# A seven-product output projection: its operand sums and the last gating bound to the order of the text, and one quad's modulation products a step sooner

## The chip, the cores and the metric

The kernel runs on one core of a Trainium2 chip. Its time is device microseconds (us) of one execution; 876.02 us is the median of three (876.01 to 876.03). The engines are PE (matrix products), DVE and ACT (element-wise work), POOL (here only DMA with accumulation) and SP (here only loads).

## The reference, cut to what matters

The input is 512 latent tokens and 256 context tokens of width 1024. Layer 0 is bidirectional retention with 4 heads, layer 1 a chunked gMLP; each is modulated by products of a conditioning vector with `ada_w`. Everything is float32. The change touches layer 0:

```python
def retention_output(o, z, w_out):                    # o: a head's scores times v, z: its gate
    o = o * lax.rsqrt(jnp.mean(o * o, axis=-1, keepdims=True) + NORM_EPS)
    o = o.transpose(0, 2, 1, 3).reshape(b, l, h * dv).astype(z.dtype)
    return (o * jax.nn.silu(z)) @ w_out
...
shift_x, scale_x, gate_x = jnp.split(silu_c @ ada_w[i] + ada_b[i], 3, axis=-1)
...
x = x + gate_x[:, None] * out_x
```

A head has 256 columns of q and k and 512 of v and z. The score of each pair of tokens is multiplied by a power of the head's decay before it meets v.

## The kernel before, in words

**Products in float32.** PE multiplies in a reduced form, so every operand is split: ACT casts it to its high half, DVE subtracts that from it to get the low half (`split`), and `mm3` adds three products (low x high, high x low, high x high). A weight tile of 1024 columns costs one ACT CAST and one DVE subtraction (hl<-raw); halves lie in four `hl` tiles, so that the preparation of weights runs two products ahead of their use (`Q.get`).

**Seven products in place of eight.** Large weights are multiplied in quads: a matrix is cut in 2 x 2, and seven products of sums replace eight of parts (`PAIRED` and `SINGLE` give their order). Weight sums T1 and T2 are made by DVE (raw<-raw), T3 and T4 by an accumulating DMA on POOL's queue. The other operand of each product is A11, A12, A22 or one of the sums S1 to S4; in the output projection of heads 0 and 1, tags stand for them: A11 in oS3, A12 in oA12, A22 in oA22, S1 in oA11, S2 in oS1, S4 in oS2, S3 in oS4. `PAIRED` there is B11 (with A11), B21 (A12), T1 (S1), T2 (S2), B22 (S4), T3 (S3), T4 (A22), each for two column pairs in turn: fourteen works, numbered n = 0 to 13. Each is a block of 24 records of 256 columns on PE. A block's result is read by `Product`: snapshots (snap) by ACT, additions to them by DVE.

**Order.** `Queue` wraps an engine: PE runs in the order of the text throughout. ACT and DVE are ordered freely by the scheduler, but inside a `pinned` stretch each instruction comes after the one before it in the text, and after a `fence` nothing later passes it. `aside(work)` runs one step of a generator pinned: such steps are loads with their halves (`load_qk`, `load_v`, `load_wo`), the decay tables (`decay`), and `step`, the next step of `background`. That one makes four vectors of modulation in turn (`ada_piece`: eight rows ada<-adag are loaded into `bg` tiles, and DVE adds each, times a number, to `ada_a`); `columns` then multiplies ada_a with ones on PE, ACT copies the result out (cole), PE transposes it. A PSUM bank has the tag "ps" (six banks) or "tm" (two).

**Attention** (`attend`): for each head, half of the tokens and pair of key blocks, a score (12 products in a tm bank), its decay (pf on DVE), its halves (ph, pl), and two steps later the products with v. `finish` squares and takes the root on ACT, `gated` multiplies with the gate on DVE (gt), `flip` transposes the gated block on PE, and `turn` makes the operands from it. Heads 0 and 1 go together (`attend_two`): a quarter of the 2 x 2 cut comes from each half. The last gated block is flipped inside the second block of the projection (`out_two`, after half of its products), and quarter_22 makes S1, S2, S4 and A22 from it at once. Heads 2 and 3 are done one by one (`attend_one`, `project_out`).

`between_modes` is one product of ones with ones between transpositions and the next products; PE shows it as two records.

The z quad of head 2 is the sixth quad (n = 5) of the loop over `QUADS[3:]`; at its products i in the step table (L1198) `step` runs.

## Time and profile before

| what | before |
|---|---|
| median of three runs | 876.02 us |
| the profiled execution | 875.56 us |
| its span in the profile | 873.8 us |
| clock of PE granted, mean | 0.995 |
| PE busy 350 to 400, 400 to 450, 450 to 500 us | 49.46, 47.33, 47.43 of 50 us |
| granted clock in the same | 1.00, 0.97, 1.00 |
| DVE busy in the same | 45.91, 34.03, 41.10 us |

The span lies inside the time of the execution; 1.76 us of the execution lie outside it. A timeline row gives start, duration, engine, what is written and read, the shape and the number of instructions; in brackets stand the idle time before it and the instruction that ended it. The projection of heads 0 and 1 takes 380.7 to 425.8 us, head 2 and its projection 426 to 476, head 3 what comes then.

### The profile page before, as it was taken

How to read it: one execution, taken by the hardware profiler on the slowest of the kernel's cores; microseconds unless marked ns; L12 is line 12 of the kernel's file. 1: busy time of each engine (PE TensorE's matmuls, PEld its weight loads, DVE VectorE, ACT ScalarE, POOL GpSimd, SP SyncE). 2: the span in 40 equal slices, each digit the busy share in tenths (PEclk: the TensorE clock that was granted, in tenths of full speed). 3: DMA queues.
4: the chain of work that ended last, by engine and by line, in shares of the span. 5: the costliest groups of instructions: out<-in, count | busy, mean ns of one | idle time of the engine just before them, and what ended most of it. 6: DMA issues, size and time to landing. Idle time of an engine off the chain costs nothing.

```text
span 873.8 us, 17037 instructions
## 1 busy us (share of the span) xinstructions
PE 856.6 (98%) x6820; PEld 818.0 (94%) x6820; DVE 709.4 (81%) x1003; ACT 479.9 (55%) x757; POOL 84.8 (10%) x127
## 2 busy tenths in 40 slices
PE   8999999999999999999999999999999999999996
PEld 7899999999999999889989899999999899899985
DVE  4799899969968875897677879998888478678895
ACT  5466544464355346657672549744666456255434
POOL 0001211211211010010100002021000000000110
PEclk9999999999999999999999999999999999999998
DMA  9945867868967796258984642657555246146532
GB/s 360 403 122 151 248 193 270 254 201 242 303 188 223 232 337 199 87 151 272 239 288 150 217 105 109 203 148 236 175 146 191 51 146 203 39 145 194 121 48 97
DMA packets 78126, 167.96 MB, mean 192 GB/s; under 512 B 8160, under 2 KB 33248, under 8 KB 78048
## 3 DMA queue, kind: packets, MB, share of 16 engines
q1 hardware_dynamic: 65280, 126.30, 43.4%
q0 software_dynamic: 12336, 40.38, 18.3%
q8 instruction: 53, 0.87, 0.4%
q10 hardware_dynamic: 432, 0.20, 0.1%
q14 instruction: 25, 0.20, 0.1%
HBM read 128.58 MB, written 24.12 MB: 175 GB/s over the span
## 4 chain that ended last, share of the span: by engine, by line
PE 81%; DVE 8%; DMA 7%; ACT 2%; issue 1%; DVEq 0%; SPq 0%; ACTq 0%
PE pst L54 81%; DMA ada_w<-in_ada_dram 2%; DVE hl L54 2%; DMA cq<-in_cT_dram 1%; DVE v L54 1%; DMA bg<-in_adag_dram 1%; DVE gt L54 1%; DMA qk<-q 1%; DMA bg<-in_dec_dram 1%; DVE ada_a L54 1%; DMA vt<-vt 1%; DVE quarter L54 1%; DMA raw<-in_w_dram 1%; DVE pf L54 0%; DMA cv<-in_cv_dram 0%
## 5 line engine op out<-in xcount | busy, mean ns | idle before, releaser
L54 DVE TENSOR_TENSOR hl<-raw,hl 128x1024 fp32r<-128x1024 f32 (+2 forms) x203 | 242.5, 1199 | 71.8 <-ACT hl L54 71.3
L54 ACT CAST hl<-raw 128x1024 fp32r<-128x1024 f32 (+2 forms) x203 | 208.3, 1031 | 155.7 <-PE pst L54 70.6
L54 PE MATMUL pst<-oS,hl 128*128 128x256 f32 x1296 | 157.4, 280 | 2.3 <-DVE hl L54 1.8
L54 PEld LDWEIGHTS pst<-oS,hl 128*128 128x128 f32 x1296 | 152.5, 190 | 3.6 <-DVE hl L54 2.1
L54 PE MATMUL pst<-hl,oS 128*128 128x256 f32 x1152 | 134.4, 276 | 0.0
L54 PE MATMUL pst<-oA,hl 128*128 128x256 f32 x1080 | 134.3, 280 | 0.1
L54 PEld LDWEIGHTS pst<-hl,oS 128*128 128x128 f32 x1152 | 132.3, 188 | 0.8 <-ACT hl L54 0.4
L54 PEld LDWEIGHTS pst<-oA,hl 128*128 128x128 f32 x1080 | 127.8, 188 | 2.0 <-ACT oS L54 0.4
L54 PE MATMUL pst<-hl,oA 128*128 128x256 f32 x768 | 92.4, 277 | 0.0
L54 DVE TENSOR_TENSOR raw<-raw 128x1024 f32<-128x1024 f32 x73 | 88.8, 1219 | 0.8
L54 PEld LDWEIGHTS pst<-hl,oA 128*128 128x128 f32 x768 | 89.4, 188 | 0.0
L54 ACT ACTIVATE snap<-pst 128x512 f32<-128x512 f32 x81 | 48.2, 595 | 63.3 <-PE pst L54 63.2
L54 PE MATMUL pst<-v,ph 128*128 128x512 f32 x192 | 59.8, 393 | 0.0
L54 PE MATMUL pst<-hl,ya 128*128 128x512 f32 (+1 forms) x246 | 59.1, 386 | 0.0
L187 POOL DMA_DIRECT2D raw<-raw x27 | 23.5, 869 | 365.1 <-DVE raw L54 145.5
L54 DVE TENSOR_TENSOR snap<-snap,pst 128x512 f32<-128x512 f32 x75 | 51.0, 680 | 6.2 <-PE pst L54 5.9
L54 PEld LDWEIGHTS pst<-hl,ya 128*128 128x128 f32 x246 | 45.3, 188 | 9.5
L54 PE MATMUL pst<-og,hl 128*128 128x256 f32 x384 | 46.6, 280 | 0.0
L54 PEld LDWEIGHTS pst<-og,hl 128*128 128x128 f32 x384 | 45.0, 188 | 0.4 <-DVE og L54 0.3
L54 PEld LDWEIGHTS pst<-v,ph 128*128 128x128 f32 x192 | 36.1, 188 | 7.1
L54 PEld LDWEIGHTS pst<-qk 128*128 128x128 f32 x288 | 35.8, 188 | 3.9 <-DVE pf L54 2.8
L54 PE MATMUL pst<-qk 128*128 128x256 f32 x288 | 36.8, 280 | 2.6 <-DVE pf L54 2.6
(222 smaller groups left out, 1085.6 us busy)
## 6 DMA issues: line engine op xcount, KB each, us to landing
raw<-in_w_dram SPq DMA_DIRECT2D x224, 256.0 KB, 3.8
bg<-in_adag_dram SPq DMA_DIRECT2D x32, 512.0 KB, 4.9
raw<-raw POOLq DMA_DIRECT2D x27, 512.0 KB, 5.1
ada_w<-in_ada_dram SPq DMA_DIRECT2D x16, 512.0 KB, 9.1
raw<-in_w_dram SPq DMA_DIRECT2D x16, 512.0 KB, 4.4
bg<-in_dec_dram SPq DMA_DIRECT2D x12, 512.0 KB, 5.1
v<-snap POOLq DMA_DIRECT2D x16, 256.0 KB, 4.4
z<-snap POOLq DMA_DIRECT2D x16, 256.0 KB, 4.6
```

What stands on the lines that cost most here:

```text
L54: made = op(*args, **kw)
L187: nc.gpsimd.dma_start(self.raws[q, to], self.raws[q, src], accum_op=ALU.add)
```

## The change

The last quarter of the seven-part projection is no longer made at once when its block is flipped: quarter_22 becomes a generator `sums`, whose four steps run pinned behind the works n = 1 (S1), 3 (S2), 5 (S4) and 6 (A22). The last gating is pinned and fenced (`bound`), and the weights that are made `ahead` of the projection are pinned too. `between_modes` moves into every flip. Head 2's decay goes to other tags and starts at n = 7; the last two halves of its v run in its own attention (`own`). The rows of the last modulation vector (i = 3) come into three tiles, loaded two ahead, and one step of `background` more is taken in the first half of head 2's projection, one less in head 3's attention. In the z quad of head 2 the second of three steps runs behind the third product instead of the fourth.

```diff
@@ -976,13 +976,13 @@
 
     row_tags = ["g0", "s3"]
 
-    def ada_piece(i, tag, tags):
+    def ada_piece(i, tag, tags, ahead=1):
         a = st([P, D], tag, name="ada_a")
         rows = []
         for k in range(KT + 1):
-            if k < KT:
+            for j in range(len(rows), min(k + ahead, KT)):
                 rows.append(bg_raw(tags))
-                load(rows[k], adag_d[8 * i + k])
+                load(rows[j], adag_d[8 * i + j])
             if k == 0:
                 yield None
                 continue
@@ -1016,7 +1016,7 @@
     def background():
         for i in range(4):
             a = None
-            for a in ada_piece(i, *(("g1", row_tags) if i < 3 else ("oA22", ("w2", "w3")))):
+            for a in ada_piece(i, *(("g1", row_tags) if i < 3 else ("oA22", ("w2", "w3", "g1"), 2))):
                 if a is None:
                     yield
             yield
@@ -1051,12 +1051,16 @@
 
     bg = background()
 
+    def bound(work):
+
+        before = act.pinned
+        act.pinned = dve.pinned = True
+        r = work()
+        act.pinned = dve.pinned = before
+        return r
+
     def aside(work):
-
-        act.pinned = dve.pinned = True
-        r = next(work, None)
-        act.pinned = dve.pinned = False
-        return r
+        return bound(lambda: next(work, None))
 
     def step():
         return aside(bg)
@@ -1195,7 +1199,7 @@
                 popped()
             if (n, i) in ((0, 3), (0, 5), (1, 0), (1, 2)):
                 aside(ctx_sum)
-            if 2 not in pieces and i in {0: (2, 4, 6), 1: (1, 3, 5, 6), 2: (1, 3, 5), 3: (0, 2, 4, 6), 5: (1, 3, 5), 6: (1, 3, 5)}.get(n, range(7)):
+            if 2 not in pieces and i in {0: (2, 4, 6), 1: (1, 3, 5, 6), 2: (1, 3, 5), 3: (0, 2, 4, 6), 5: (1, 2, 5), 6: (1, 3, 5)}.get(n, range(7)):
                 pieces.append(step())
             if n == 3 and i % 2:
                 aside(dec0)
@@ -1270,7 +1274,8 @@
             act.activation(ss, ss, AF.Sqrt, bias=eps, scale=1.0 / 512)
             due.append(lambda: gated(h, hf, ss))
             if (h, hf) == end:
-                due.pop(0)()
+                bound(due.pop(0))
+                dve.fence()
 
         def gated(h, hf, ss):
             dve.reciprocal(ss, ss)
@@ -1291,6 +1296,7 @@
                         o = b * HS + t * P
                         pe.transpose(pq[:, o:o + P], gts[t][:, (2 * fp + b) * P:(2 * fp + b) * P + P], ident)
                 flipped.append(pq.rearrange("p (b t) -> p b t", b=2))
+            between_modes()
             turn(h, hf, flipped)
 
         LAG = 2
@@ -1312,7 +1318,7 @@
             run((i, 2))
         return flip
 
-    def attend_one(h, qs, vs, wo, steps):
+    def attend_one(h, qs, vs, wo, steps, own=()):
 
         og = [st([P, 2, 4, HS], tag, F32R, name="og") for tag in ("oS3", "oS4")]
 
@@ -1324,6 +1330,8 @@
         plan = {(5, 0): [of(qs), of(wo)]}
         for i in range(8):
             plan[i, 2] = [of(qs)] + ([of(vs)] if i > 4 else []) + ([of(wo)] if i < 5 else []) + ([step] if i in steps else [])
+        for i in range(2):
+            plan[i, 2] += [of(work) for work in own]
         return og, attend((h,), plan, turn)
 
     def attend_two(qs, vs, ds, q2):
@@ -1353,9 +1361,10 @@
                 split((t[:, 0, k, :], t[:, 1, k, :]), src)
 
         def turn(h, hf, flipped):
-            act.pinned = dve.pinned = True
-            (quarter_11, quarter_21, quarter_12, quarter_22)[2 * h + hf](flipped)
-            act.pinned = dve.pinned = False
+            if (h, hf) == (1, 1):
+                last.append(flipped)
+            else:
+                bound(lambda: (quarter_11, quarter_21, quarter_12)[2 * h + hf](flipped))
 
         def quarter_11(flipped):
             halved_parts("A11", flipped)
@@ -1374,17 +1383,24 @@
             for r, x, src in zip(plain("12", "g1"), parts("11"), flipped):
                 dve.tensor_tensor(r, x, src, ALU.subtract)
 
-        def quarter_22(flipped):
+        last = []
+
+        def sums():
+            flipped = last.pop()
             for r, src in zip(parts("21"), flipped):
                 dve.tensor_tensor(r, src, r, ALU.subtract)
             halved("S1", at["21"])
+            yield
             for r, src in zip(parts("11"), flipped):
                 dve.scalar_tensor_tensor(r, src, -1.0, r, ALU.mult, ALU.subtract)
             halved("S2", at["11"])
+            yield
             for r, src in zip(parts("12"), flipped):
                 dve.tensor_tensor(r, src, r, ALU.add)
             halved("S4", at["12"])
+            yield
             halved_parts("A22", flipped)
+            yield
 
         def raws():
             Q.limit, Q.stage = FIRST_V1, 2
@@ -1396,14 +1412,14 @@
             Q.pump()
 
         def ahead(n):
-            return lambda: aside(iter([Q.upto(PROJECTED + n)]))
+            return lambda: bound(lambda: Q.upto(PROJECTED + n))
 
         of = lambda work: lambda: aside(work)
         q, v, d, q2 = of(qs), of(vs), of(ds), of(q2)
         plan = {(0, 2): [q, q, q, d], (1, 2): [d, v], (2, 2): [d, q, v], (3, 2): [q, q, v], (4, 1): [q], (5, 2): [v],
                 (6, 2): [q, v, q2, q2, q2], (7, 1): [v, raws], (8, 1): [v], (10, 1): [q2, q2],
-                (11, 2): [more, ahead(1)], (12, 2): [q2, ahead(2)]}
-        return attend((0, 1), plan, turn)
+                (11, 2): [more, ahead(1)], (12, 2): [ahead(2)], (13, 2): []}
+        return attend((0, 1), plan, turn), sums()
 
     def out_two(flip, works):
 
@@ -1415,17 +1431,13 @@
                     act.activation(acc[:, m, th * HS:th * HS + HS], t[:, s * HS:s * HS + HS], AF.Copy, scale=gate0[:, m:m + 1])
             return done
 
-        def turned():
-            flip()
-            between_modes()
-
         prods = {q: Product(outward, put(q[1])) for q in OUT0}
         n = 0
         for name in PAIRED:
             for q in OUT0:
                 w = Q.get()
                 if n == 1:
-                    inside.append(turned)
+                    inside.append(flip)
                 prods[q].run(name, w)
                 for work in works.get(n, ()):
                     aside(work)
@@ -1445,7 +1457,7 @@
                         prepare()
                 for work in parts:
                     aside(work)
-                if then is None and hf == 1:
+                if then is None and (hf == 1 or c == 3):
                     step()
                 for mi in range(2):
                     m = 2 * c + mi
@@ -1455,24 +1467,25 @@
                     for kk in range(4):
                         o = kk * 256 + mi * P
                         mm3(p, (w[:, 0, o:o + P], w[:, 1, o:o + P]), (og[hf][:, 0, kk, :], og[hf][:, 1, kk, :]), kk == 0, kk == 3)
-                        if (hf, m, kk) == (0, 4, 1) and then is None:
-                            between_modes()
                     dve.scalar_tensor_tensor(acc[:, m, sl], p, gate0[:, m:m + 1], acc[:, m, sl], ALU.mult, ALU.add)
                     if then:
                         then(hf, m)
 
     hls[0] += -hls[0] % HL
-    qs, ds, vs = load_qk(2), decay(2, ("w3", "g1")), load_v(2)
-    flip = attend_two(load_qk(1), load_v(1), decay(1, ("w3", "g1")), qs)
-    out_two(flip, {6: (vs, ds), 8: (vs, qs), 9: (ds,), 10: (vs, qs), 11: (vs, ds), 12: (vs, qs), 13: (vs, vs)})
+    qs, vs = load_qk(2), load_v(2)
+    flip, ss = attend_two(load_qk(1), load_v(1), decay(1, ("w3", "g1")), qs)
+    ds = decay(2, ("s0", "s2"))
+    out_two(flip, {1: (ss,), 3: (ss,), 5: (ss,), 6: (vs, ss), 7: (ds,), 8: (vs, qs), 9: (ds, qs), 10: (vs, vs, qs), 11: (ds,),
+                   12: (vs,)})
     drained(ds)
     drained(qs)
-    drained(vs)
+    own = vs
     Q.limit = None
     qs, vs = load_qk(3), load_v(3)
-    og, flip = attend_one(2, qs, vs, load_wo(2), (2, 3, 5, 6))
+    og, flip = attend_one(2, qs, vs, load_wo(2), (2, 3, 5, 6), (own,))
+    drained(own)
     project_out(wos.pop(2), og, flip, (decay(3, ("s0", "s2")), vs, qs))
-    og, flip = attend_one(3, iter(()), iter(()), load_wo(3), (0, 1, 2, 3, 5, 6))
+    og, flip = attend_one(3, iter(()), iter(()), load_wo(3), (1, 2, 3, 5, 6))
     for _ in bg:
         pass
```

In the z quad of head 2 PE's order changes at one place (24 products a block; oA_570 is the operand of B21, oS_1239 that of T3; ada_a x ones are the modulation products):

```order
 L54 MATMUL pst<-hl,oS_861 128x256 x24
 L54 MATMUL pst<-hl,oS_1012 128x256 x24
-L54 MATMUL pst<-hl,oA_570 128x256 x24
 L54 MATMUL pst<-ada_a,ones 32x256 x4
+L54 MATMUL pst<-hl,oA_570 128x256 x24
 L54 MATMUL pst<-hl,oS_1239 128x256 x24
 L54 MATMUL pst<-hl,oS_1173 128x256 x24
```

The modulation products moved ahead of B21's block. ACT's order around the copy of their result (cole_3201), in the changed kernel:

```order
L54 CAST hl_3203<-raw_2644 128x1024
L54 ACTIVATE snap_3194<-pst_3107 128x512
L54 CAST hl_3238<-raw_2850 128x1024
L54 COPY cole_3201<-pst_3196 128x256
L54 CAST hl_3274<-raw_2898 128x1024
```

The copy stands behind the cast of a weight tile there. DVE in the seven-part projection, before, from S2's low half (oS1) to the low half of the weights T2 of the second column pair (hl_5000; quarter_4777 is what becomes S4, oS2 S4's low half):

```order
L54 TENSOR_TENSOR oS1_4872<-quarter_4507,oS1_4872 128x1024
L54 TENSOR_TENSOR quarter_4777<-pst_4855,quarter_4777 128x512
L54 TENSOR_TENSOR quarter_4777<-pst_4860,quarter_4777 128x512
L54 TENSOR_TENSOR snap_4899<-snap_4899,pst_4939 128x512
L54 TENSOR_TENSOR hl_4968<-raw_4545,hl_4968 128x1024
L54 TENSOR_TENSOR oS2_4877<-quarter_4777,oS2_4877 128x1024
L54 TENSOR_TENSOR oA22_4880<-pst_4855,oA22_4880 128x512
L54 TENSOR_TENSOR oA22_4880<-pst_4860,oA22_4880 128x512
L54 TENSOR_TENSOR raw_4547<-raw_4745,raw_4547 128x1024
L54 TENSOR_TENSOR hl_5030<-raw_4743,hl_5030 128x1024
L54 TENSOR_TENSOR hl_5070<-raw_4745,hl_5070 128x1024
L54 TENSOR_TENSOR hl_5000<-raw_4547,hl_5000 128x1024
```

And in the changed kernel, from S1's low half (oA11) to the same weights (hl_4994; quarter_4509 is what becomes S2, oS1_4958 S2's low half):

```order
L54 TENSOR_TENSOR oA11_4887<-quarter_4656,oA11_4887 128x1024
L54 TENSOR_TENSOR snap_4840<-snap_4840,pst_4895 128x512
L54 TENSOR_TENSOR hl_4924<-raw_4549,hl_4924 128x1024
L54 TENSOR_TENSOR raw_4547<-raw_4747,raw_4547 128x1024
L54 TENSOR_TENSOR snap_4883<-snap_4883,pst_4928 128x512
L54 SCALAR_TENSOR_TENSOR quarter_4509<-pst_4859,quarter_4509 128x512
L54 SCALAR_TENSOR_TENSOR quarter_4509<-pst_4864,quarter_4509 128x512
L54 TENSOR_TENSOR hl_4962<-raw_4547,hl_4962 128x1024
L54 TENSOR_TENSOR raw_4549<-raw_4749,raw_4549 128x1024
L54 TENSOR_TENSOR oS1_4958<-quarter_4509,oS1_4958 128x1024
L54 TENSOR_TENSOR hl_5029<-raw_4747,hl_5029 128x1024
L54 TENSOR_TENSOR hl_4994<-raw_4549,hl_4994 128x1024
```

S2 and the second column pair's T2 weights stand closer together now: S2's low half moved to two steps ahead of these weights, where S4 and A22 stood. Last, DVE ahead of the third score of head 3 (pf on dt), before, with the rows of the last modulation vector (ada_a<-bg) and the additions of head 2's projection (acc):

```order
L54 SCALAR_TENSOR_TENSOR acc_4237<-pst_5776,gate0_895,acc_4237 128x256
L54 SCALAR_TENSOR_TENSOR acc_4237<-pst_5790,gate0_895,acc_4237 128x256
L54 SCALAR_TENSOR_TENSOR acc_4237<-pst_5807,gate0_895,acc_4237 128x256
L54 SCALAR_TENSOR_TENSOR ada_a_5396<-bg_5742,cpad_175,ada_a_5396 128x1024
L54 SCALAR_TENSOR_TENSOR acc_4237<-pst_5821,gate0_895,acc_4237 128x256
L54 SCALAR_TENSOR_TENSOR ada_a_5396<-bg_5773,cpad_175,ada_a_5396 128x1024
L54 SCALAR_TENSOR_TENSOR acc_4237<-pst_5838,gate0_895,acc_4237 128x256
L54 SCALAR_TENSOR_TENSOR acc_4237<-pst_5852,gate0_895,acc_4237 128x256
L54 SCALAR_TENSOR_TENSOR ada_a_5396<-bg_5804,cpad_175,ada_a_5396 128x1024
L54 SCALAR_TENSOR_TENSOR pf_5881<-pst_5868,dt_5587 128x512
```

And in the changed kernel:

```order
L54 SCALAR_TENSOR_TENSOR ada_a_5402<-bg_5567,cpad_175,ada_a_5402 128x1024
L54 SCALAR_TENSOR_TENSOR acc_4237<-pst_5772,gate0_895,acc_4237 128x256
L54 SCALAR_TENSOR_TENSOR ada_a_5402<-bg_5724,cpad_175,ada_a_5402 128x1024
L54 SCALAR_TENSOR_TENSOR acc_4237<-pst_5789,gate0_895,acc_4237 128x256
L54 SCALAR_TENSOR_TENSOR acc_4237<-pst_5803,gate0_895,acc_4237 128x256
L54 SCALAR_TENSOR_TENSOR ada_a_5402<-bg_5755,cpad_175,ada_a_5402 128x1024
L54 SCALAR_TENSOR_TENSOR acc_4237<-pst_5818,gate0_895,acc_4237 128x256
L54 SCALAR_TENSOR_TENSOR acc_4237<-pst_5832,gate0_895,acc_4237 128x256
L54 SCALAR_TENSOR_TENSOR ada_a_5402<-bg_5786,cpad_175,ada_a_5402 128x1024
L54 SCALAR_TENSOR_TENSOR acc_4237<-pst_5847,gate0_895,acc_4237 128x256
L54 SCALAR_TENSOR_TENSOR acc_4237<-pst_5861,gate0_895,acc_4237 128x256
L54 SCALAR_TENSOR_TENSOR pf_5890<-pst_5877,dt_5597 128x512
```

Four rows stand there in place of three, the last two additions now between the last row and pf; each row has at least one addition ahead of it.

## The prediction

> **What bounds the kernel now.** I read the page first (busy shares, chain), then the timeline of PE for the places where it stands still, then DVE and ACT there, and the clock by windows.
>
> ```profile
> PE 856.6 (98%) x6820; PEld 818.0 (94%) x6820; DVE 709.4 (81%) x1003; ACT 479.9 (55%) x757; POOL 84.8 (10%) x127
> PE 81%; DVE 8%; DMA 7%; ACT 2%; issue 1%; DVEq 0%; SPq 0%; ACTq 0%
> ...
> 550.00:600.00 50.00, 50.00 (x443) 49.99 (x442) 48.40 (x63) 29.23 (x37) 6.66 (x11) 1.00 0.67 204
> ```
>
> PE is the bound: in an undisturbed stretch 443 products of 256 columns fill 50 us, so one costs 0.113 us and a block of 24 costs 2.72. The change removes no product, so only what PE waits for can be won. PE at the places that the diff touches (start, length, count; a wait stands in brackets):
>
> ```profile
> 240.85 2.88 PE L54 MATMUL pst<-hl,oA 128*128 128x256 f32 x24
> 244.51 0.64 PE L54 MATMUL pst<-ada_a,ones 128*32 128x256 f32 x8 [0.78 <-DVE snap L54]
> 245.08 5.71 PE L54 MATMUL pst<-hl,oS 128*128 128x256 f32 x48
> 250.63 0.38 PE L54 MATMUL pst<-ident,cole 128*128 128x128 f32 x2
> 250.85 0.39 PE L54 MATMUL pst<-ones 128*128 128x128 f32 x2
> ...
> 380.73 4.25 PE L54 MATMUL pst<-oS,hl 128*128 128x256 f32 x36
> 385.25 0.30 PE L54 MATMUL pst<-ident,gt 128*128 128x128 f32 x1 [0.27 <-DVE gt L54]
> 385.82 0.98 PE L54 MATMUL pst<-ident,gt 128*128 128x128 f32 x7 [0.27 <-DVE gt L54]
> ...
> 388.27 11.47 PE L54 MATMUL pst<-oA,hl 128*128 128x256 f32 x96
> 399.58 2.99 PE L54 MATMUL pst<-oS,hl 128*128 128x256 f32 x24
> 404.42 15.93 PE L54 MATMUL pst<-oS,hl 128*128 128x256 f32 x120 [1.85 <-DVE hl L54]
> 420.18 5.82 PE L54 MATMUL pst<-oA,hl 128*128 128x256 f32 x48
> ...
> 431.06 0.50 PE L54 MATMUL pst<-v,pl 128*128 128x512 f32 x1 [0.83 <-DVE pl L54]
> ...
> 476.03 2.88 PE L54 MATMUL pst<-qk 128*128 128x256 f32 x24
> 481.48 1.65 PE L54 MATMUL pst<-qk 128*128 128x256 f32 x12 [2.56 <-DVE pf L54]
> ```
>
> Every gap here ends with a DVE result. The dearest stands in the seven-part output projection: its eighth block (T2 of the second column pair) waits until 404.42 for the low half of its weights, and then five blocks take 15.76 us (404.42 to 420.18) where 5 x 2.72 = 13.6 are due. The clock column, ahead of DMA share and GB/s, says why:
>
> ```profile
> 404.00:405.00 1.00, 0.58 (x4) 0.59 (x5) 1.00 (x2) 0.14 (x1) 0.00 (x0) 0.87 0.96 229
> 405.00:406.00 1.00, 1.00 (x6) 1.00 (x6) 0.49 (x1) 0.24 (x1) 0.00 (x0) 0.50 1.11 254
> ```
>
> After the wait PE runs at half clock. The 2.2 us missing are 1.7 of that (3.4 us at half) and small waits.
>
> **z quad (term 1, a loss).** The products ones x ada_a now stand ahead of B21. Before, they stood after it and waited for DVE to empty a bank. These and the quad's T1 and B21 results share two banks (tag tm), and T1's stays full until B22: so now B21 must wait until ACT has copied the modulation products out (COPY cole). ACT's queue there, and the copy's length:
>
> ```profile
> 241.54 1.04 ACT L54 CAST hl<-raw 128x1024 fp32r<-128x1024 f32 x1
> ...
> 246.66 0.35 ACT L54 COPY cole<-pst 128x256 f32<-128x256 f32 x1
> ```
>
> In the new order the copy is behind that cast: it runs from 242.55 to 242.9. The modulation products start at 240.95 and take 0.57 (244.51 to 245.08), so B21 could start at 241.5 and starts at 242.9; it takes 2.72, and T3 starts at 245.6 instead of 245.08: **+0.55**. Bounds: were the copy ahead of the cast, the wait would go and T3 start at 244.3 (-0.8); with half a clock after it, +2.2. I take the row's order. What stands behind PE is every later product, so this counts in full.
>
> **Mode products (term 2, a loss).** Each transposition of a gated block now ends with between_modes, two short records: 250.63 to 250.85 shows 0.11 a record. Six flips gain one (three in the attention of heads 0 and 1, one in head 2's, two for head 3; the eighth and head 2's second had one): 6 x 0.22 = **+1.3**, on PE and so in full. Should the switch to the next product become shorter by it, the least is about 0.
>
> **Seven-part projection (term 3).** I lay the new DVE order against DVE's own spacing:
>
> ```profile
> 384.36 1.40 DVE L54 SCALAR_TENSOR_TENSOR gt<-pst,ss,z 128x512 f32<-128x512 f32 x2
> 385.68 1.21 DVE L54 TENSOR_TENSOR hl<-raw,hl 128x1024 fp32r<-128x1024 f32 x1
> 386.81 1.28 DVE L54 TENSOR_TENSOR quarter<-pst,quarter 128x512 f32<-128x512 f32 x2
> 388.01 1.21 DVE L54 TENSOR_TENSOR raw<-raw 128x1024 f32<-128x1024 f32 x1
> ...
> 400.88 4.62 DVE L54 TENSOR_TENSOR hl<-raw,hl 128x1024 fp32r<-128x1024 f32 x4
> ...
> 382.46 0.29 ACT L54 ACTIVATE ss<-ss,eps 128x2 f32<-128x2 f32 x1
> ```
>
> Wide steps follow each other by 1.14 (four in 4.62, the last 1.21 long), narrow ones by 0.60 (386.81 to 388.01), the two gt by 1.32. Three more mode products put PE 0.66 later at 381.4. The last gating waits for ACT's root, now at 383.1 (382.46 + 0.66), so its gt pair runs from 383.6 to 384.95; before, two weight halves ran ahead of it. PE's 36 products end at 385.5, and the transpositions no longer wait. With them (0.9), their mode product (0.2) and twelve products (1.45) the third block starts at 388.05 instead of 388.27; four blocks as before (11.3) lead to 399.4.
>
> There it needs S2's low half (oS). From 384.95 DVE has ten wide and six narrow steps to do before it: 11.4 + 3.6 gives 399.95, and it ends at 401.15: **a wait of 1.75 stays**, at another operand. Blocks seven and eight then run to 406.6. S4's low half comes after three wide steps, two narrow, one wide and half of A22: 399.95 + 3.4 + 1.2 + 1.14 + 0.6 = 406.3, done at 407.5: **0.9 more**. Without half clock the thirteenth block starts at 407.5 + 2.6 + 3 x 2.72 = 418.3 instead of 420.18: **-1.9** (0.66 of term 2 is inside; 0.66 is left of it).
>
> Does the clock fall again? It fell at 404.74 (0.87 in that us). If it is judged in stretches as long as the low one, 3.4 us, edges lie at 401.33 and 397.9; S2's wait, 0.55 later by term 1, lies from 399.95 to 401.7, across an edge, with under 1.4 on either side. I take no half clock.
>
> The Trainium skill (TensorE: Matmul & The Clock Gate, Part 1) lets the clock fall only after an idle window of about 3.4 us. The trace disagrees: 1.85 us of waiting was enough; it agrees on how long it stays low. By that rule the rival of the half clock below has no chance; by the rows it keeps one.
>
> **Start of head 2 (term 4).** Before, two halves of v stood between the first score and its low half on DVE:
>
> ```profile
> 428.06 2.35 DVE L54 TENSOR_TENSOR v<-v 128x1024 fp32r<-128x1024 f32 x2
> 430.33 0.68 DVE L54 TENSOR_TENSOR pl<-pf,ph 128x512 fp32r<-128x512 f32 x1
> ```
>
> They now stand after pl, one by one; PE's scores end at 429.9 and its first product with v started at 431.06: **-1.1**. Less would be won if the second half came late for the second product, 4.1 us on; DVE has 2.3 to do there.
>
> **Modulation rows (term 5).** DVE's queue ahead of the third score of head 3, and two loads from the chain:
>
> ```profile
> 466.12 0.69 DVE L54 TENSOR_TENSOR dt<-bg 128x512 f32<-128x512 f32 x1 [1.64 <-ACT bg L54]
> ...
> 469.39 1.27 DVE L54 SCALAR_TENSOR_TENSOR ada_a<-bg,cpad,ada_a 128x1024 f32<-128x1024 f32 x1
> ...
> 474.47 1.28 DVE L54 SCALAR_TENSOR_TENSOR ada_a<-bg,cpad,ada_a 128x1024 f32<-128x1024 f32 x1 [1.83 <-DMA bg<-in_adag_dram]
> ...
> 479.54 1.28 DVE L54 SCALAR_TENSOR_TENSOR ada_a<-bg,cpad,ada_a 128x1024 f32<-128x1024 f32 x1 [1.41 <-DMA bg<-in_adag_dram]
> 480.74 0.68 DVE L54 SCALAR_TENSOR_TENSOR pf<-pst,dt 128x512 f32<-128x512 f32 x1
> ...
> 458.46 6.20 DMA bg<-in_dec_dram
> 470.69 3.68 DMA bg<-in_adag_dram
> ```
>
> With two buffers each load waits for a product and DVE for the load. Now there are three, with loads two ahead. Up to here PE and DVE are 2.8 earlier (-1.9 - 1.1 + 0.2). So the first ada_a runs at 466.6, the next two at 468.2 and 469.8 on rows long there. The last two rows are loaded after the first two products (467.85 and 469.4) and land 3.68 later (471.5, 473.1); with two acc between each pair, the products run at 471.8 and 473.8, and pf from 475.8 to 476.5. The third score could start at 473.25 + 2.72 = 475.95: 0.55 of wait is left of 2.75 (481.48 less 476.03 + 2.72): **-2.2**. With 6.20 a load, pf ends at 478.8 and nothing is won; with loads that land at once, 2.75.
>
> **Sum**: +0.55 - 1.9 - 1.1 + 0.66 - 2.2 = -4.0. The profiled execution took 875.56 (span 873.8), 0.46 under the median 876.02; I set the difference against the median: **872.0**.
>
> **Rivals.**
> 1. *Half clock returns.* The new waits are as long as the old one; if one falls inside one stretch, 1.7 is lost again. S4's wait (0.9) may hide part of it, or move with it, since the cast of S4's half stands behind the slow block's snapshot: 0.8 to 1.7, I take 1.5: 873.5. For it: 1.85 sufficed. Against: the edge above. 15%.
> 2. *The loads are as slow as the 6.20 row*: term 5 is lost, 874.2. Against: both adag loads in that chain took 3.7. 8%.
> 3. *The bound order does not do what it says*: S2 comes as late as the weights did, since DVE's list is the same length; term 3 gives nothing, 873.9. Against: the gt pair and head 2's v halves do leave the list. 7%.
> 4. *Slower: three waits in place of one.* S1's low half ends at 393.05 (five wide, two narrow and itself from 384.95), needed at 393.5: 0.45 to spare. If the root comes behind one more cast and subtraction, 2 us late, then S1, S2 and S4 each hold PE by nearly 2 us, each with half a clock: 2 + 3 x 1.7 = 7.1, 879.1. It decides once the gating is over 0.45 late and each wait over 1.8. Against: the order puts only one cast ahead of the root. 6%.
>
> **Chances and range.** The forecast itself (871.0 to 873.0) has 54%, rivals 1 to 3 alone 30%: all of these lie over 0.2% under the time before (1.75 us, so below 874.27; about what a measurement of this kernel can tell from no change), so faster has 84%. Two of them together give about the time before (1 and 2: 875.7; 2 and 3: 876.1): same 10%. Slower 6%. The range's low end is the forecast less the 1.35 between the row's order and the lower bound of term 1 (+0.55 to -0.8) and 0.45 of the last 0.55 of term 5: 870.2. Its high end, 874.4, stands just over rival 2.
>
> **What would show it.** In the changed profile: PE's wait at T2 moved to its first block, under 2.1 us, on an oS half, then a smaller one at B22; clock 1.00 in all windows there; a wait of 1.4 ahead of B21 on ACT cole near 242; no wait at the first v,pl; under 1 us ahead of head 3's third score; six more pairs of ones records. A clock of 0.50 after 400, or ada_a waiting over 3 us for a row, would make the number wrong.

## The result, and the profile after

The changed kernel takes 870.81 us (median of four runs, 870.39 to 871.6), the kernel before 876.01 in the same comparison: a ratio of 0.9944 with a 95% interval of 0.9926 to 0.9961. A second measurement gave 871.15 (0.994, 0.992 to 0.996). The profiled execution took 871.02, its span is 868.7, 5.1 under that of before.

The page of the changed kernel, busy time and the chain that ended last:

```profile
PE 855.8 (99%) x6832; PEld 817.9 (94%) x6832; DVE 709.0 (82%) x1003; ACT 480.0 (55%) x757; POOL 84.8 (10%) x127
...
PE 92%; DMA 3%; DVE 3%; ACT 1%; issue 1%; DVEq 0%; SPq 0%; ACTq 0%
```

PE has twelve records more (the six pairs), and the chain, 81% PE before, is 92% PE now: DVE's and DMA's steps have left it. PE's timeline at the places of the prediction:

```profile
240.78 0.64 PE L54 MATMUL pst<-ada_a,ones 128*32 128x256 f32 x8
242.74 3.00 PE L54 MATMUL pst<-hl,oA 128*128 128x256 f32 x24 [1.32 <-ACT cole L54]
245.58 5.61 PE L54 MATMUL pst<-hl,oS 128*128 128x256 f32 x48
...
385.35 1.03 PE L54 MATMUL pst<-ident,gt 128*128 128x128 f32 x8
...
387.86 11.70 PE L54 MATMUL pst<-oA,hl 128*128 128x256 f32 x96
399.39 0.28 PE L54 MATMUL pst<-oS,hl 128*128 128x256 f32 x1
401.04 5.73 PE L54 MATMUL pst<-oS,hl 128*128 128x256 f32 x48 [1.37 <-DVE oS L54]
407.38 11.04 PE L54 MATMUL pst<-oS,hl 128*128 128x256 f32 x95 [0.61 <-DVE oS L54]
418.25 5.60 PE L54 MATMUL pst<-oA,hl 128*128 128x256 f32 x48
...
427.77 0.39 PE L54 MATMUL pst<-v,pl 128*128 128x512 f32 x1
...
473.11 4.60 PE L54 MATMUL pst<-qk 128*128 128x256 f32 x36
```

The starts of the same work, laid against those of before, give the account of the gain. T3 of the z quad starts at 245.58, where before it was 245.08. The thirteenth block of the projection starts at 418.25 (before: 420.18), head 2's first product with v at 427.77 (431.06), head 3's scores at 473.11 (476.03), and the third of them follows without a bracket, where 2.56 stood. The clock in the two new waits stays full (length, busy time and count of PE, weight loads, DVE, ACT and POOL, then granted clock, DMA share, GB/s):

```profile
400.00:401.00 1.00, 0.00 (x0) 0.00 (x0) 1.00 (x2) 1.00 (x3) 0.62 (x1) 1.00 1.08 221
401.00:402.00 1.00, 0.96 (x8) 0.96 (x9) 1.00 (x1) 1.00 (x2) 0.22 (x1) 1.00 1.07 213
...
407.00:408.00 1.00, 0.62 (x5) 0.62 (x6) 1.00 (x3) 0.99 (x3) 0.00 (x0) 1.00 1.01 381
```

### The profile page after: what moved, and what is told of

Same layout as the page of the kernel before. It is cut to its first block, busy times and chain, and to the rows that moved or that the text cites. A ratio compares the mean times of both kernels' runs of the same rounds, so it can differ in the third digit from the quotient of the medians.

```text
span 868.7 us, 17054 instructions
## 1 busy us (share of the span) xinstructions
PE 855.8 (99%) x6832; PEld 817.9 (94%) x6832; DVE 709.0 (82%) x1003; ACT 480.0 (55%) x757; POOL 84.8 (10%) x127
## 4 chain that ended last, share of the span: by engine, by line
PE 92%; DMA 3%; DVE 3%; ACT 1%; issue 1%; DVEq 0%; SPq 0%; ACTq 0%
PE pst L54 92%; DMA ada_w<-in_ada_dram 2%; DVE hl L54 1%; DMA cq<-in_cT_dram 1%; DMA cv<-in_cv_dram 1%; DVE raw L54 0%; DVE quarter L54 0%; ACT junk L54 0%; DVE o L54 0%; DVE oS L54 0%; DVE snap L54 0%; ACT hl L54 0%; ACT fss L54 0%; DVE gt L54 0%; DVE oA L54 0%
## 5 line engine op out<-in xcount | busy, mean ns | idle before, releaser
L54 PE MATMUL pst<-oS,hl 128*128 128x256 f32 x1296 | 155.2, 278 | 2.0 <-DVE oS L54 2.0
L54 PEld LDWEIGHTS pst<-oS,hl 128*128 128x128 f32 x1296 | 150.4, 188 | 3.3 <-DVE oS L54 2.4
L54 PE MATMUL pst<-v,pl 128*128 128x512 f32 x96 | 37.6, 391 | 0.0
```

Of the source, the lines that this page charges most:

```text
L54: made = op(*args, **kw)
```

## The experiments

Each was compared with the kernel before on the same chip. The changed kernel, once more among them, is the yardstick. The experiments ran on three chips, A, B and C, and the kernel before has another median on each: between chips the ratios compare, not the times.

| kernel | median us | before there (chip) | ratio to before (95%) |
|---|---|---|---|
| changed, first | 870.81 | 876.01 | 0.9944 (0.9926 to 0.9961) |
| changed, again | 871.15 | 876.98 (A) | 0.9940 (0.9920 to 0.9960) |
| z step back | 870.86 | 876.67 (A) | 0.9941 (0.9921 to 0.9961) |
| ones back | 869.90 | 876.67 (A) | 0.9931 (0.9907 to 0.9955) |
| sums at once, gating free | 874.20 | 876.67 (A) | 0.9974 (0.9961 to 0.9987) |
| rows back | 873.10 | 876.67 (A) | 0.9960 (0.9945 to 0.9975) |
| halves of v back | 872.64 | 876.98 (A) | 0.9953 (0.9937 to 0.9970) |
| other bank for ones x ada_a | 870.13 | 876.98 (A) | 0.9925 (0.9897 to 0.9953) |
| gating free | 869.93 | 876.98 (A) | 0.9925 (0.9896 to 0.9953) |
| sums at once, gating bound | 875.15 | 875.30 (B) | 1.0004 (0.9988 to 1.0020) |
| three edits together | 868.47 | 875.30 (B) | 0.9918 (0.9901 to 0.9935) |
| and one row later | 867.00 | 875.30 (B) | 0.9905 (0.9887 to 0.9924) |
| and ones six products later | 867.34 | 876.72 (C) | 0.9892 (0.9870 to 0.9914) |

Only the two kernels with the sums at once, and the last two, have an interval that lies beside one of the changed kernel's two or touches its edge. For the others the times alone don't tell them from it, and what is said of single places rests on the traces.

### The z quad's step back

```diff
-            if 2 not in pieces and i in {..., 5: (1, 2, 5), ...}.get(n, range(7)):
+            if 2 not in pieces and i in {..., 5: (1, 3, 5), ...}.get(n, range(7)):
```

> The changed kernel, but the z quad's second step runs behind its fourth product again, so that ones x ada_a stands after B21. Theory: the wait moves from ACT's copy (1.32 ahead of B21 in the changed kernel) back to DVE's emptying of a bank (0.78 ahead of the modulation products before the change), and the whole kernel is 0.5 us faster than the changed one (870.3). Rival (the change in this quad is what makes the first 250 us no slower, by loads that come sooner): slower than the changed kernel by 0.5 or more. A third: nothing but PE's wait moves, its end within 0.2.

At its place the first theory held: B21 starts without a wait, the modulation products wait for DVE again, and T3 starts at 244.92, 0.66 before the changed kernel's 245.58 (0.55 from its next record on).

```profile
240.69 2.88 PE L54 MATMUL pst<-hl,oA 128*128 128x256 f32 x24
244.35 0.64 PE L54 MATMUL pst<-ada_a,ones 128*32 128x256 f32 x8 [0.78 <-DVE snap L54]
244.92 1.29 PE L54 MATMUL pst<-hl,oS 128*128 128x256 f32 x9
```

The whole did not follow: 870.86. In its profile the lead of 0.66 was gone long before the projection: a load of q landed later (ACT waited 2.26 for it at 313 us, 1.07 in the changed kernel), and from 314 to 363 us PE's products of 256 columns ran at an interval of 0.1178 us, which in the changed kernel only those from 328 to 349 did; at 359 PE was 0.33 behind the changed kernel. So the change's step is a loss at its place, and too small to be seen in the time.

### Another bank for the modulation products

```diff
     def columns(a, dst):
-        pr = pt((P, HS), tag="tm")
+        pr = pt((P, HS))
```

> The changed kernel with the products ones x ada_a in a bank of tag ps in place of tm. Theory (the wait of 1.32 ahead of B21 is for its bank, that the copy empties): the wait is gone, 1.4 to 2.1 of the excess at 240 to 243 us, and the kernel is 1.3 to 2.1 faster at that place; of it some may be given back where DVE sets the pace (the wait on S2's low half, 1.65, grows only if DVE's list does not start sooner too). 869.0 to 869.8. Rival (B21 waits for its weights or anything else the cast behind it makes): the wait stays at 1.3, time as the changed kernel.

ACT's queue in the changed kernel shows the order that the prediction read from the listing: the copy behind the cast, and B21 0.05 after the copy's end (242.69).

```profile
241.38 1.04 ACT L54 CAST hl<-raw 128x1024 fp32r<-128x1024 f32 x1
242.31 0.38 ACT L54 COPY cole<-pst 128x256 f32<-128x256 f32 x1
```

With the other bank, PE's timeline has no wait there:

```profile
241.66 0.64 PE L54 MATMUL pst<-ada_a,ones 128*32 128x256 f32 x8
242.23 3.00 PE L54 MATMUL pst<-hl,oA 128*128 128x256 f32 x24
```

So the wait was for the bank, as the first theory said: the products follow 0.57 behind one another. The time, 870.13, is 0.7 to 1.0 under the changed kernel, less than the 1.39 won at the place, above the 869.0 to 869.8 that was expected, and inside the overlap of the intervals. In this profile PE had come to the place 0.88 later than in the changed kernel's, 0.5 of it already at 26 us.

### Ones x ones where it was

```diff
                 flipped.append(pq.rearrange("p (b t) -> p b t", b=2))
-            between_modes()
             turn(h, hf, flipped)
...
+        def turned():
+            flip()
+            between_modes()
...
-                    inside.append(flip)
+                    inside.append(turned)
...
+                        if (hf, m, kk) == (0, 4, 1) and then is None:
+                            between_modes()
```

> The changed kernel without the ones x ones product in the flips, and with it where it stood before (behind the last flip of heads 0 and 1, and six products behind the first flip of head 2's projection). Theory A (the six pairs only cost): 12 records fewer, 1.3 us faster, 869.5, less in the seven-part projection, where a DVE result is waited for and takes 0.4 to 0.7 of it: 869.5 to 870.1. Theory B (PE has two cadences, 0.1133 and 0.1178 us a product of 256 columns, and where the pair stands behind a transposition decides which holds afterwards): the stretch of head 2's projection goes at 0.1133 in place of 0.1178 (0.8 us in 22 us), and other stretches change too: over 1.5 us faster, or slower where a stretch falls into the slow cadence; shown by the interval between products in the trace, not by the sum of waits.

869.9. At the places each missing pair is 0.22, as theory A has it. But the trace shows theory B too: the interval between products of 256 columns is 0.1133 us in some stretches and 0.1178 in others, at a granted clock of 1.00 in both, and where a stretch changes is not the same as in the changed kernel. The last experiment returns to it.

### Sums and binding: four kernels

The seven-part edit has two halves: the sums spread over the works, and the last gating bound and fenced. Sums at once and gating free:

```diff
             if (h, hf) == end:
-                bound(due.pop(0))
-                dve.fence()
+                due.pop(0)()
...
-            if (h, hf) == (1, 1):
-                last.append(flipped)
-            else:
-                bound(lambda: (quarter_11, quarter_21, quarter_12)[2 * h + hf](flipped))
+            bound(lambda: (quarter_11, quarter_21, quarter_12, quarter_22)[2 * h + hf](flipped))
...
-    out_two(flip, {1: (ss,), 3: (ss,), 5: (ss,), 6: (vs, ss), 7: (ds,), 8: (vs, qs), 9: (ds, qs), 10: (vs, vs, qs), 11: (ds,),
+    out_two(flip, {6: (vs,), 7: (ds,), 8: (vs, qs), 9: (ds, qs), 10: (vs, vs, qs), 11: (ds,),
```

> The changed kernel with the operand sums of the last quarter made at once again and its last gating bound to no place; head 2's and head 3's edits stay. Theory: the transpositions wait again (about 0.5), and T2 of the second column pair waits for its weights again (1.9), in place of waits of 1.65 and 0.88 on S2 and S4: about the same sum of waits, and slower than the changed kernel by what the half clock (1.7) and the slow cadence after it (0.8) cost, 1.5 to 3 us: 872.3 to 873.8. Rival (the order of the sums itself is the gain, waits shrink with it): the half clock stays away and the waits alone make it 1 to 2 us slower. Rival (the binding does nothing): within 0.5 of the changed kernel.

874.2, above the 872.3 to 873.8 that was expected. PE waited for the weights again, and longer than before the change. Behind its row stand two windows of PE alone (us, busy, granted clock, DMA share, GB/s):

```profile
406.36 5.84 PE L54 MATMUL pst<-oS,hl 128*128 128x256 f32 x49 [2.41 <-DVE hl L54]
...
404.00:406.00 2.00, 0.00 (x0) 1.00 1.01 414
406.00:408.00 2.00, 1.64 (x14) 1.00 1.09 290
```

The half clock, expected by the theory, did not come in this profile, though the wait was longer than the 1.85 after which it came before. So this profile does not show what half clock costs this kernel; the waits alone put the works behind them 1.8 later than in the changed kernel, and over 1 more was lost around head 2's first transpositions.

Gating free, sums at their works (the first of the three pieces of that diff alone):

> The changed kernel with the last gating bound to no place; the sums stay at their works. DVE then does three wide steps of weights ahead of the two gt, and fewer behind. Theory (DVE's list up to S2's low half is what counts, and it is equally long): the transpositions wait 0.5 to 1 again, the wait on S2's low half gets shorter by the same, and the time stays within 0.4 of the changed kernel, if no half clock falls in. Rival (the gating's place is the gain): S2's wait stays at 1.6 or more and the kernel is 0.5 to 1 slower.

Both expectations missed: the wait on S2 went altogether. DVE around the gating, of the changed kernel:

```profile
379.17 1.29 DVE L54 TENSOR_TENSOR oA<-pst,oA 128x512 fp32r<-128x512 f32 x2 [2.53 <-ACT oA L54]
...
383.31 0.17 DVE L54 RECIPROCAL ss<-ss 128x2 f32<-128x2 f32 x1 [0.52 <-ACT ss L54]
383.51 1.41 DVE L54 SCALAR_TENSOR_TENSOR gt<-pst,ss,z 128x512 f32<-128x512 f32 x2
...
399.77 1.22 DVE L54 TENSOR_TENSOR oS<-quarter,oS 128x1024 fp32r<-128x1024 f32 x1
```

And of the kernel with the gating free:

```profile
379.08 1.23 DVE L54 TENSOR_TENSOR hl<-raw,hl 128x1024 fp32r<-128x1024 f32 x1 [0.79 <-ACT hl L54]
...
383.82 1.21 DVE L54 TENSOR_TENSOR hl<-raw,hl 128x1024 fp32r<-128x1024 f32 x1
384.94 1.41 DVE L54 SCALAR_TENSOR_TENSOR gt<-pst,ss,z 128x512 f32<-128x512 f32 x2
...
397.86 1.23 DVE L54 TENSOR_TENSOR oS<-quarter,oS 128x1024 fp32r<-128x1024 f32 x1
```

Bound, DVE stood still for 2.53 and 0.52 ahead of the gating; free, for 0.79, since weight halves fill the time. S2's low half comes 1.91 sooner, and PE's timeline has no wait on S2 or S4 left, only the one at the transpositions:

```profile
386.40 0.98 PE L54 MATMUL pst<-ident,gt 128*128 128x128 f32 x7 [0.33 <-DVE gt L54]
...
400.17 17.12 PE L54 MATMUL pst<-oS,hl 128*128 128x256 f32 x144
```

The thirteenth block starts at 417.13 in place of 418.25, though PE was 0.4 later at the projection's start. The time is 869.93, 0.9 to 1.2 lower, inside the overlap of the intervals: 0.9 of it is given back at head 3's third score.

Sums at once, gating bound (the other pieces of that diff):

> The changed kernel with the sums at once again, but the last gating bound and fenced: the fourth of four (sums at their works or at once, gating bound or free). Theory (binding the gating makes DVE stand still for the root, some 2 to 3 us of its time, and DVE's list sets PE's waits): slower than the sums at once with free gating, 874.2, by 1 to 2 us: 875 to 876. Rival (the bound gating only costs together with the spread sums): 874.2 or less.

875.15, against 874.2 with the gating free; by the ratios, since the chips differ, 1.0004 against 0.9974, which is 2.6 us. PE waits twice at blocks ahead of S2, and then the clock falls:

```profile
395.22 3.06 PE L54 MATMUL pst<-oA,hl 128*128 128x256 f32 x24 [1.19 <-DVE snap L54]
400.32 4.55 PE L54 MATMUL pst<-oA,hl 128*128 128x256 f32 x24 [2.04 <-DVE snap L54]
...
400.00:402.00 2.00, 1.68 (x8) 1.68 (x9) 2.00 (x3) 2.00 (x4) 0.91 (x2) 0.55 0.78 268
402.00:404.00 2.00, 2.00 (x12) 2.00 (x12) 2.00 (x4) 2.00 (x4) 0.77 (x1) 0.59 1.10 207
```

The four ratios are 0.9940 to 0.9944 (spread, bound), 0.9925 (spread, free), 0.9974 (at once, free) and 1.0004 (at once, bound). Spreading the sums is worth 4.3 us with the gating free, with intervals apart. Binding the gating costs 1.3 to 1.7 by the ratios with the sums spread, inside the overlap of the intervals, and 2.6 with the sums at once, where the intervals just miss each other. The traces are narrower. From the projection's start to its thirteenth block PE takes 36.99 (spread, bound), 35.48 (spread, free), 38.19 (at once, free) and 39.76 (at once, bound, of which 1.7 is half clock), and 39.45 before (1.7 of it too). So spreading gains 2.7 there with the gating free, and binding costs 1.5 with the sums spread. With the sums at once, binding costs nothing there but the half clock, and that hangs on where a wait falls (see the account of the prediction).

### The halves of v, and the modulation rows

```diff
-    out_two(flip, {..., 9: (ds, qs), 10: (vs, vs, qs), 11: (ds,), 12: (vs,)})
+    out_two(flip, {..., 9: (ds, qs), 10: (vs, qs), 11: (vs, ds), 12: (vs,), 13: (vs, vs)})
+    drained(vs)
...
-    own = vs
+    own = iter(())
```

> The changed kernel with the halves of head 2's v made inside the seven-part projection again, at the works where they stood. Theory: they stand between the first score of head 2 and its low half again, and PE waits about 1.1 for the first product with v; the works 11 to 13 have DVE time left, so nothing else moves: 1.1 slower than the changed kernel (871.9). Rival (that wait came from head 2's decay table, which also moved): no wait there, within 0.3 of the changed kernel.

The wait returned with its cause: two halves of v on DVE between the first score's pf and its pl, and PE behind pl.

```profile
426.67 2.35 DVE L54 TENSOR_TENSOR v<-v 128x1024 fp32r<-128x1024 f32 x2
428.94 0.69 DVE L54 TENSOR_TENSOR pl<-pf,ph 128x512 fp32r<-128x512 f32 x1
...
429.68 0.50 PE L54 MATMUL pst<-v,pl 128*128 128x512 f32 x1 [0.83 <-DVE pl L54]
```

The time is 1.5 to 1.8 higher; 1.1 of it is this wait.

```diff
-            for a in ada_piece(i, *(("g1", row_tags) if i < 3 else ("oA22", ("w2", "w3", "g1"), 2))):
+            for a in ada_piece(i, *(("g1", row_tags) if i < 3 else ("oA22", ("w2", "w3")))):
...
-                if then is None and (hf == 1 or c == 3):
+                if then is None and hf == 1:
...
-    og, flip = attend_one(3, iter(()), iter(()), load_wo(3), (1, 2, 3, 5, 6))
+    og, flip = attend_one(3, iter(()), iter(()), load_wo(3), (0, 1, 2, 3, 5, 6))
```

> The changed kernel with the last modulation vector as before: two tiles, loads one ahead, no step in the first half of head 2's projection, one step more in head 3's attention. Theory: the third score of head 3 waits 2.5 to 3 us again, 2.2 to 2.8 slower than the changed kernel (873.0 to 873.6). Rival (the gain at that place comes from the earlier start of everything ahead of it): the wait is under 1.5, and the time under 872.3.

```profile
479.16 1.65 PE L54 MATMUL pst<-qk 128*128 128x256 f32 x12 [2.52 <-DVE pf L54]
```

873.1, and the wait at head 3's third score is back at 2.52, though PE came to these scores within 0.54 of the changed kernel: the rows made the gain, not the earlier start.

### The changed kernel again

> The changed kernel once more, for the spread from run to run: 870.8. The waits of the seven-part projection (1.65 and 0.88) and of the z quad (1.3) the same within 0.1; what moves by over 0.3 is where loads land. If the half clock hangs on where its windows of 3.4 us fall, the runs of the kernel before have a lower mean clock (0.995) than these (0.998), and those with the lower clock are the longer ones.

871.15. The chain of waits of this second profile, and PE at head 3's third score:

```profile
430.49 5.71 DMA raw<-in_w_dram
...
455.05 7.20 DMA bg<-in_dec_dram
...
469.87 4.67 DMA bg<-in_adag_dram
...
477.37 1.65 PE L54 MATMUL pst<-qk 128*128 128x256 f32 x12 [1.61 <-DVE pf L54]
```

The same program waits 1.61 here where the first profile showed none: the loads took 7.20 (6.20 in the prediction's row) and 4.67 (3.68), as the prediction's second rival had it, in part. The waits on S2 and S4 were the same within 0.1. The mean granted clock of the runs of the changed kernel was 0.998 (ten runs, 0.997 to 0.999), that of the kernel before 0.995 (59 runs beside these experiments, 0.991 to 0.999); among those 59 the 12 with a clock of 0.993 or less took 877.4 on average, the 15 with 0.997 or more 874.8.

### Together, and one row later

The gating free, the other bank and the ones as before, in one kernel:

> The changed kernel with three edits of the runs so far together: the last gating free, ones x ada_a in a bank of tag ps, ones x ones where it stood before the change. Theory (the three are at three places): at the places 1.8 + 1.4 + 0.9 = 4.1 us less than the changed kernel up to head 2's attention; but the third score of head 3 waits for DVE, whose rows wait for loads, so 1.5 to 2 of it is given back there: 868.5 to 869.5. Rival (DVE and the loads set the end of head 2 altogether): no faster than the best single one, 869.9 to 870.1.

868.47, at the edge of what the first theory gave. Its parts do not come out: PE starts head 2's scores at 420.58, 3.1 and not 4.1 ahead of the changed kernel, since it ran the whole projection at the slow interval. The give-back came, at head 3's third score:

```profile
474.10 1.65 PE L54 MATMUL pst<-qk 128*128 128x256 f32 x12 [1.67 <-DVE pf L54]
```

The ratio, 0.9918, is within the spread of the best single ones (0.9925), so the time does not exclude the rival. The last row ahead of that score was then moved behind it:

```diff
-                if then is None and (hf == 1 or c == 3):
+                if then is None and (hf == 1 and c < 3 or (hf, c) == (0, 3)):
...
-    og, flip = attend_one(3, iter(()), iter(()), load_wo(3), (1, 2, 3, 5, 6))
+    og, flip = attend_one(3, iter(()), iter(()), load_wo(3), (1, 2, 3, 4, 5, 6))
```

> The same three edits, and the row of modulation that stands last ahead of head 3's third score moved behind it (one step less in the second half of head 2's projection, one more in head 3's attention). Theory: the row and its wait for a load (1.3 and 0.2 to 1.4) no longer stand ahead of pf, and the third score waits under 0.4: 1 to 1.7 faster than the three edits without it, 867 to 868. Rival (the decay table ahead of it sets pf): the wait stays; or the row turns up as a wait in head 3's later gating, and the time is the same.

867.0, the lowest median. It is 1.5 under the kernel without this step, as expected, though the intervals overlap; the third score follows its predecessors without a wait, all 36 products in one group:

```profile
471.61 4.24 PE L54 MATMUL pst<-qk 128*128 128x256 f32 x36
```

### Where the pair of ones stands

Against the kernel of one row later:

```diff
-            if kt == 2 and inside:
+            if kt > 1 and inside:
                 inside.pop(0)()
...
-                    inside.append(turned)
+                    inside.extend((flip, between_modes))
```

> The kernel with one row later, and the ones x ones product of the seven-part projection six products behind the last flip in place of directly behind it. The same number of records; in that run PE was in the slow cadence (0.1178 us a product of 256 columns) from 383 to 455 us, without a wait of over 0.6 in it up to 440. Theory (PE's cadence is set where a short product stands; six products behind a flip it left the fast one in head 2's projection): 0.1133 holds from 386 on, the 336 products of 256 columns up to 426 take 1.5 us less, and of it some is given back where DVE sets the pace: 0.5 to 1.5 faster than with one row later, 865.5 to 866.5. Rival (the place of the pair does not set the cadence): the interval stays 0.1178 there, and the time 867.0.

A window of 10 us of the projection, first with the pair directly behind the flip, then six products later (PE's count first, its granted clock third from the end):

```profile
400.00:410.00 10.00, 10.00 (x87) 10.00 (x86) 8.51 (x11) 9.32 (x15) 0.00 (x0) 1.00 1.00 332
```

```profile
400.00:410.00 10.00, 10.00 (x90) 10.00 (x90) 9.16 (x12) 9.83 (x15) 0.00 (x0) 1.00 0.99 330
```

87 products against 90 in the same time, PE busy throughout and at full clock: the first theory on the cadence. From 387 us to head 2's first transposition PE gained 1.6; there it waited 0.59 longer for DVE. The time, 867.34, is above the 865.5 to 866.5 that was expected. It comes from another chip than 867.0; the ratio is 0.0013 (1.1 us) lower, inside the overlap of the intervals, so the gain is seen in the trace alone.

## Why the prediction was right, point by point

**Forecast -4.0, measured -5.2.** The sign and the range held. By place, start against start in the two profiles:

- **z quad: +0.55 forecast, +0.5 measured** (0.4 from T3's second record on). Both the mechanism (B21 behind ACT's copy behind a cast) and the size; the lower bound, no wait, is what the other bank gave.
- **Mode pairs: 0.22 each, as forecast.** That they could also set PE's cadence was not in the working.
- **Seven-part projection: -1.9 forecast with its three pairs.** From T3 of the z quad to the thirteenth block the lead grew by 2.43; 0.54 of that is a load of q at 314 us that came sooner in the second profile (ACT waited 1.07 for it in place of 2.75), so -1.9 is left. S2's wait was put at 1.75 and came to 1.65 between the records around it, S4's at 0.9 and came to 0.88 (the brackets, 1.37 and 0.61, leave out the pipelined end of the product ahead). Most of the -1.9, 1.7, is the half clock that the profile before had and this one has not: the waits themselves did not shrink (1.85 before, 1.65 and 0.88 now). And binding the gating, which was to spare the transpositions a wait, was a loss: DVE stood still for 3.05, and without it S2 comes without a wait. The DVE list was laid from its spacing alone; that a pinned gating also keeps ready weight halves behind it was not priced. Rival 3 asked whether the bound order does what it says, and looked for the answer in the list's length.
- **Half clock: right for a reason that does not hold.** The working put edges of 3.41 us by one profile and set S2's wait across one. Two profiles have a low stretch inside the program, and in both the clock falls again when PE has ended: 404.75 to 868.96 is 136.0 stretches of 3.41, 400.21 to 871.25 is 138.0. So the edges of one execution stand on one grid. But edges carried over from the first profile to the second would be 397.9, 401.3 or 404.7: they lie elsewhere in each execution. The Trainium skill (TensorE: Matmul & The Clock Gate, Part 1) calls the window free-running, with a phase that differs from run to run; these profiles agree with that. On the changed kernel's own grid, reckoned back from 866.05, S2's wait lies inside one stretch, 398.42 to 401.84, and not across an edge. PE in single stretches of the own grids (busy, granted clock, DMA share, GB/s): a fall and the stretch ahead of it, before and with sums at once and gating bound; then the stretch with the 2.41 wait, and that with the changed kernel's wait on S2.

```profile
401.33:404.74 3.41, 1.56 (x13) 1.00 1.01 324
404.74:408.16 3.42, 3.42 (x18) 0.50 0.95 249
...
396.80:400.21 3.41, 1.48 (x13) 1.00 0.96 352
400.21:403.62 3.41, 3.29 (x15) 0.50 0.91 231
...
404.70:408.11 3.41, 1.75 (x15) 1.00 1.05 334
...
398.42:401.84 3.42, 2.05 (x17) 1.00 1.01 262
```

The clock fell behind stretches in which PE was busy 46% and 43%, and stayed behind 51% and 60%; behind one of 52%, at head 3's third score before, it stayed too. So it need not be idle for a whole stretch. What kept the clock up in the changed kernel is that its two waits are short and 6 us apart: 1.37 of idle leaves 60% of a stretch wherever it lies. The 2.41 wait was cut by an edge at 404.70, and a wait as long as that is safe by its place alone.

- **Start of head 2: -1.1 forecast, -1.1 measured** (from 425.84 against 423.69 to 431.06 against 427.77), and the wait came back with the two halves.
- **Modulation rows: -2.2 forecast, -2.5 measured in the first profile.** 0.55 of wait was to be left; none was, but PE came to the place later than it would have at the fast cadence, which hid it. In the second profile 1.61 was left, and the place gained 1.0. The size hangs on loads of 3.7 to 7.2, and rival 2 was this. That the first profile gave the forecast's size is in part luck. The working also left the z quad's 0.55 out of the 2.8 by which PE was to be ahead here; it measured 2.92, with 0.54 of it from the load of q.
- **What the sum lacked.** Loads that differ from run to run moved 0.54 at 314 and 0.6 at 653 us in favour of the changed kernel's profile; neither is the change's. A slow stretch from 546 to 564 us cost it 0.6. So the total's nearness to the forecast is in part luck too.
- **A misreading of before.** Of the 2.2 missing in five blocks, 1.7 was half clock, and the rest was put down to small waits. It was the slow cadence: thirteenth and fourteenth block took 5.82 there and 5.60 in the changed kernel, with no wait in either.

The terms undone one by one cost 0, -1, +3, +1.7 and +2.2 against the changed kernel, together about 6; the gain was 5.2 in the first comparison and 5.8 in the second, so the sum is the gain within the spread. That a later place takes back what an earlier one frees is seen in the traces, at head 3's third score: 0.85 with the gating free, 1.67 with three edits.

## What to carry to other kernels

Bind an instruction to its place only after asking what ready work the engine would do in its stead: the spread sums were worth some 4 us, and the pinned gating beside them cost over 1. A wait is worth what the next place does not take back, so look there before counting it; the row moved behind head 3's third score paid only because that score was the next thing to wait. And compare profiles start against start by place: one profile's load times decide half a microsecond here and there.

## What the runs showed of the hardware that was not expected

PE runs these products at one of two steady intervals, 0.1133 and 0.1178 us for 256 columns, both at a granted clock of 1.00. A slow stretch lasts from under one to seventy us and more, and begins or ends at a group of short products, at a wait or at a single longer interval. With one pair of ones six products later it was gone over 60 us, from 386 to 447. One profile each would prove little, but the others bear it out: in all 13 with the pair directly behind the last flip, the blocks behind it start at the slow interval. Behind the first flip of head 2's projection the slow one follows in 6 of 9 profiles with the pair directly there, and in none of the 5 with it six products later. Why the one place gives the fast interval and the other the slow one was not found; the same program also differed between two profiles (head 2's projection at 0.1178 in the first, at 0.1133 in the second).

The clock fell to half for 3.41 us after a wait of 1.85, and stayed full after one of 2.41. What decided in these profiles is PE's busy share of one stretch on a grid of 3.41 us that is fixed within an execution: over all 14 profiles it fell behind 46% and less, and behind no stretch of 49% or more. Two of the falls met work, at 43 and 46%; the others came at the program's end.
